# The last 1536 gate columns of the modulation, as running sums on VectorE beside the output projection

## The chip, the cores and the metric

The kernel runs on one core of one Trainium2 chip, in one launch. The metric is the device time of that launch in microseconds (us); lower is better. It is given as the median of several runs, and one further execution is recorded by the profiler.

## The reference

One layer of a diffusion backbone: 384 tokens (128 of a prompt, 256 of a sample) of width 4096, all in float32. A conditioning vector gives shift, scale and gate for the prompt and for the sample; the tokens are normalised and modulated, projected to the inputs of eight retention heads and sixteen delta-rule heads, mixed, and projected back; the gate scales the result before it is added to the tokens.

```python
mod = jax.nn.silu(c) @ w_ada[l] + b_ada[l]           # 2 vectors (c_ctx, c) x [4096, 12288]
shift, scale, gate = jnp.split(mod, 3, axis=-1)
u = _rms_norm(h, norm_w[l]) * (1.0 + scale) + shift
out, states = _mixer(u, ...)                         # u @ w_in, heads, mixed @ w_out
h = h + gate * out
y = _rms_norm(h, final_norm_w)
```

The change concerns the last third of `w_ada`: gate = silu(c) @ w_ada[:, 8192:12288] + b_ada, 4096 columns for two vectors.

## The kernel before

PE (TensorE) does nearly all of the work; a program written in Python sets the order of every instruction on every engine. The unit of this order is a piece, with a `prepare` (loads and splitting) and a `compute` (matmuls). `run_pieces` (L348) calls `prepare` for pieces ahead of the one that computes, until four of them are held (`RING - 1`), so the loads, ACT's and VectorE's steps for a piece stand ahead of its matmuls by up to four chunks.

Stages, in order of time: shift and scale beside the first parts of the input projection (0 to about 790 us); the rest of the input projection in eight pairs of heads, each with its delta-rule and retention steps as background work between the matmuls (about 790 to 2800); the output projection (about 2800 to 3328); the last norm and the stores.

*Products.* float32 products are made of three float32r matmuls. Each chunk of weights (128 rows, 512 columns) is loaded by SP into a `raw` tile that holds two chunks (`load_piece`, L193; four such tiles, `RAW_RING`), cast by ACT into `wh` (L210), and VectorE subtracts to get `wl` (L211): this is called a split here. There are five `wh` and five `wl` buffers (`RING`). In a `Gemm` of kind N the three matmuls L265, L266 and L267 form a triple; a chunk takes three triples, one for each 128 tokens.

*Output projection.* Eight blocks of 512 columns, each a `Gemm` over 32 chunks (L1320). At the end of a block, `rest` (L1300) adds three steps for each 128 tokens on VectorE, `to` (times the gate, L1303), `to`+`xo` (the tokens, L1305) and `hw` (times the norm's weight, L1307), and a square on ACT (L1308); the background clock places them between the next block's splits. The place where one block ends and the next begins is called a joint. `pre` (L1284), five chunks before a block's end, has POOL load `go` (the gate, from `d_gate` in DRAM), `wo` and `xo`. In block 0 the mixed rows are read back from DRAM (`mixl`, L1244) and split into `uh` and `ul` (L1247, L1248), two at a time.

*Gate before.* `Ada` (L302): for 512 columns there are 16 pieces; each loads 512 rows of 256 columns (512 KB, into a `raw` tile) and runs four matmuls of 128x32 by 128x256 in four column groups of the array, with the conditioning vectors (`cst`) as the stationary side (L323). Then ACT copies the sums (L1177), two matmuls with `sel` add the four groups (L1183), POOL loads the bias into `gsb` (L1187), VectorE adds (L1190), POOL stores to `d_gate` (L1191). All eight such blocks lie in the mixer stage, one in each of the eight pairs of heads 0 to 7, spread between the pieces of the kind-N groups (L1213 to L1232).

*Background.* Each pair's delta-rule (`gdn`) and retention (`ret`) steps are generators; `slot` (L186) counts the nominal time of the matmuls issued and takes the next step when the count runs out, and `pace` (L152) shrinks the counts when a due time comes near. `urgent` steps, among them the end of a gate block, go first.

Of the kernel before, what the change touches and what calls it, by code (L numbers as in the profile page):

```python
# [7 lines left out]
F32 = mybir.dt.float32  # L8
# [7 lines left out]
D = 4096  # L16
NK = 32
# [49 lines left out]
def hybrid_step(ctx: ExitStack, tc: tile.TileContext, x_prompt, x_sample, state_ret_fwd, state_ret_bwd,  # L67
# [41 lines left out]
    gnw = mid.tile([128, 1], F32, name="gnw")  # L109
    cst = mid.tile([128, 2 * NK + 32], F32, name="cst")  # L110
    sel = mid.tile([128, 2], F32, name="sel")
# [79 lines left out]


    def load_piece(src, chunks, k0, nk, ring=None):  # L193
        shape = [128, nk, len(chunks), chunks[0][1]]
        if ring:
            raw = ring(shape)
        else:
            raw = wpool.tile(shape, F32, tag="raw", name="raw", bufs=RAW_RING)
        for i, (c0, cn) in enumerate(chunks):
            SP.dma_start(out=raw[:, :, i, :],  # L200
                         in_=src[k0 * 128:(k0 + nk) * 128, c0:c0 + cn].rearrange("(k p) n -> p k n", p=128))
        return raw

    def split_tile(raw, shape, place=None):
        if place:
            h, lo = place
        else:
            h = wpool.tile(shape, F32R, tag="wh", name="wh", bufs=RING)
            lo = wpool.tile(shape, F32R, tag="wl", name="wl", bufs=RING)
        A.copy(h, raw)  # L210
        V.tensor_tensor(lo, raw, h.bitcast(F32), op=ALU.subtract)  # L211
        return h, lo

# [88 lines left out]
    class Ada:  # L302
# [14 lines left out]
        def compute(self, i, raw):  # L317
# [30 lines left out]
    def run_pieces(pieces):  # L348
# [8 lines left out]
        room = {"do": len(pieces), "ada": ADA_RING - 1, "w": RING - 1}  # L357
        kind = lambda o: "do" if isinstance(o, Do) else ("ada" if isinstance(o, Ada) and o.ring else "w")
        for idx, (obj, i) in enumerate(pieces):
# [853 lines left out]
    ada_q = []  # L1213
    for i in range(8):
        ada_q += Ada(2 * D + 512 * i, 512, lambda: ps_main.tile([128, 512], F32, tag="mm3", name="adg"), gate_done(i)).pieces
    for g, (kind, chunks) in enumerate(groups):
# [5 lines left out]
        if kind == "T":  # L1222
            pieces += gm.pieces
        else:
            n, rest = len(gm.pieces), 0
            if g % 2:
                rest = min(8, n // 2)
                cnt = len(ada_q) - 16 * (7 - g // 4)
            else:
                cnt = min(16, max(0, 16 * n // (n + NK - reached.get(g + 1, 0) - 8)))  # L1230
            pieces += gm.pieces[:LEAD] + interleave(gm.pieces[LEAD:n - rest], ada_q[:cnt]) + gm.pieces[n - rest:]
            ada_q = ada_q[cnt:]  # L1232
# [16 lines left out]


    oc = {}

# [27 lines left out]
    def out_done(c0):  # L1280
# [33 lines left out]
    def place(i):  # L1314
# [3 lines left out]
                           for t in (uh, ul)]  # L1318

    for i in range(8):  # L1320
        pre, done = out_done(512 * i)
# [6 lines left out]
        if i == 0:  # L1328
# [4 lines left out]
            for j, piece in enumerate(seq):  # L1333
                for m, fn in ((j - 2, mix_put), (j, mix_load)):
                    if 0 <= m < NK:
                        pieces += Do(lambda m=m, fn=fn: fn(m)).pieces
                pieces.append(piece)
        else:
            pieces += gm.pieces
    run_pieces(pieces)  # L1340
# [52 lines left out]
```

## Time and profile before

| | |
|---|---|
| three timed runs, us | 3339.26 (median), 3338.48 to 3340.51 |
| the profiled execution, us | 3342.99 |
| its span, first to last instruction, us | 3340.9 |
| mean granted clock of TensorE | 0.994 |
| loaded and stored | 626.14 MB, mean 187 GB/s |

In the rows below, L is the line of the kernel's source, PE the matmuls of TensorE, PEld its weight loads, DVE VectorE, ACT ScalarE, POOL GpSimd and SP the engine that issues the weight loads. A group row gives line, engine, operation, output and inputs, shapes and count, then the busy time in us and the mean of one in ns, then the idle time before them and what ended it. A timeline row gives start, length, engine, line and operation; in brackets stands the idle time before it and what it waited for. A row of waits gives who waited for whom, the total in us, how often, and the longest. A row of loads gives the tile and source, the issuing queue, the count, the size and the median time from issue to landing in us.

### The profile page before, as it was taken

The page shows a single profiled execution, that of the slowest core. Times are in us where ns is not written, and L with a number is a line of the kernel's source. Part 1 is how long each engine was busy: PE and PEld are TensorE (multiplying, and loading weights), DVE is VectorE, ACT ScalarE, POOL GpSimd, SP SyncE. Part 2 cuts the span into 40 slices and gives each one's busy share as a digit, 9 for nine tenths or more (in the row PEclk, how much of TensorE's full clock was granted, in tenths as well). Part 3 has the DMA queues.
Part 4 walks back from the last instruction along what each step waited for, and adds up shares of the span by engine and source line. Part 5 has one row for each costly group of instructions (what it writes and reads, how often), then busy time and mean ns, then how long its engine had stood idle before and what let it go on. Part 6 is the DMA issues. An engine that isn't in the chain of part 4 may idle for free. (4 is left out here: it accounts for less than half of the span.)

```text
span 3340.9 us, 51824 instructions
## 1 busy us (share of the span) xinstructions
PE 3256.4 (97%) x19312; PEld 2706.2 (81%) x19312; DVE 1840.7 (55%) x3811; ACT 1198.9 (36%) x2588; POOL 292.2 (9%) x463
## 2 busy tenths in 40 slices
PE   5999999999999999999999999999999999999998
PEld 2778888877699779789789779779779877788887
DVE  2554433335855756754856746746844845444444
ACT  3322222224245235244345245235244334333333
POOL 0000000001101001001011001011000012100000
PEclk9999999999999999999999999999999999999999
DMA  9888998975534554544645645554644556645444
GB/s 304 290 287 272 330 311 266 297 251 159 179 105 135 169 153 149 179 145 140 192 146 152 185 129 156 173 154 147 177 153 141 160 153 188 187 145 170 145 151 170
DMA packets 594236, 626.14 MB, mean 187 GB/s; under 512 B 38978, under 2 KB 577042, under 8 KB 593984
## 3 DMA queue, kind: packets, MB, share of 16 engines
q1 hardware_dynamic: 570096, 551.04, 52.7%
q0 software_dynamic: 23888, 71.79, 7.3%
q8 instruction: 151, 2.47, 0.3%
q14 instruction: 101, 0.83, 0.1%
HBM read 590.37 MB, written 32.33 MB: 186 GB/s over the span
## 5 line engine op out<-in xcount | busy, mean ns | idle before, releaser
L211 DVE TENSOR_TENSOR wl<-raw,wh 128x512 fp32r<-128x512 f32 x1274 | 854.3, 687 | 939.8 <-ACT wh L210 935.8
L210 ACT CAST wh<-raw 128x512 fp32r<-128x512 f32 x1274 | 756.6, 620 | 1350.6 <-DMA raw<-in_w_in_dram 659.0
L265 PE MATMUL mm<-wh,uh 128*128 128x512 f32 x1920 | 784.3, 408 | 9.1 <-ACT rawt L564 5.6
L266 PE MATMUL mm<-wl,uh 128*128 128x512 f32 x1920 | 755.3, 393 | 6.4 <-DVE wl L211 5.8
L267 PE MATMUL mm<-wh,ul 128*128 128x512 f32 x1920 | 752.9, 392 | 0.0
L259 PE MATMUL mm<-uh,wh 128*128 128x384 f32 x2048 | 721.0, 352 | 6.2 <-DVE ul L555 3.8
L261 PE MATMUL mm<-uh,wl 128*128 128x384 f32 x2048 | 689.4, 337 | 0.0
L260 PE MATMUL mm<-ul,wh 128*128 128x384 f32 x2048 | 688.8, 336 | 0.0
L265 PEld LDWEIGHTS mm<-wh,uh 128*128 128x128 f32 x1920 | 362.2, 189 | 141.0 <-issue 48.2
L259 PEld LDWEIGHTS mm<-uh,wh 128*128 128x128 f32 x2048 | 387.3, 189 | 51.2 <-issue 34.6
L266 PEld LDWEIGHTS mm<-wl,uh 128*128 128x128 f32 x1920 | 362.7, 189 | 81.2 <-DVE wl L211 14.1
L267 PEld LDWEIGHTS mm<-wh,ul 128*128 128x128 f32 x1920 | 362.2, 189 | 78.2 <-DVE ul L1248 0.7
L260 PEld LDWEIGHTS mm<-ul,wh 128*128 128x128 f32 x2048 | 387.6, 189 | 3.9 <-issue 2.9
L261 PEld LDWEIGHTS mm<-uh,wl 128*128 128x128 f32 x2048 | 386.8, 189 | 0.0
L854 DVE TENSOR_TENSOR tmp<-M 48x4 f32<-48x4 f32 (+14 forms) x240 | 189.3, 789 | 3.4
L323 PE MATMUL ada<-adar,cst 128*32 128x256 f32 x2048 | 147.5, 404 | 26.9 <-DMA adar<-in_w_ada_dram 26.9
L645 DVE SCALAR_TENSOR_TENSOR acc<-rawt,cw,acc 128x126 f32<-128x126 f32 (+3 forms) x384 | 133.8, 413 | 12.8 <-ACT acc L640 12.8
L266 PE MATMUL o<-wl,uh 128*128 128x512 f32 x354 | 138.1, 390 | 0.2 <-DVE wl L211 0.2
L265 PE MATMUL o<-wh,uh 128*128 128x512 f32 x354 | 138.0, 390 | 0.2 <-ACT wh L210 0.2
L267 PE MATMUL o<-wh,ul 128*128 128x512 f32 x354 | 137.9, 390 | 0.0
L323 PEld LDWEIGHTS ada<-adar,cst 128*32 128x32 f32 x2048 | 53.8, 112 | 92.7 <-DMA adar<-in_w_ada_dram 42.8
L856 DVE TENSOR_REDUCE M<-tmp 48x2 f32<-48x4 f32 (+14 forms) x240 | 121.6, 507 | 8.3
(321 smaller groups left out, 2522.7 us busy)
## 6 DMA issues: line engine op xcount, KB each, us to landing
raw<-in_w_in_dram SPq DMA_DIRECT2D x1028, 256.0 KB, 3.6
adar<-in_w_ada_dram SPq DMA_DIRECT2D x256, 512.0 KB, 5.7
raw<-in_w_ada_dram SPq DMA_DIRECT2D x128, 512.0 KB, 4.3
raw<-in_w_out_dram SPq DMA_DIRECT2D x256, 256.0 KB, 3.1
rawt<-d_part POOLq DMA_DIRECT2D x26, 384.0 KB, 4.3
d_part<-spill POOLq DMA_DIRECT2D x9, 768.0 KB, 7.4
gr<-d_gc POOLq DMA_DIRECT2D x16, 384.0 KB, 7.4
d_mix<-rawt POOLq DMA_DIRECT2D x32, 192.0 KB, 2.8
```

The source lines that it names most:

```text
L210: A.copy(h, raw)
L211: V.tensor_tensor(lo, raw, h.bitcast(F32), op=ALU.subtract)
L259: PE.matmul(ps, wh, high(k), start=st, stop=False)
L260: PE.matmul(ps, wh, low(k), start=False, stop=False)
L261: PE.matmul(ps, wl, high(k), start=False, stop=sp)
L265: PE.matmul(ps, a, h, start=st, stop=False)
L266: PE.matmul(ps, a, lo, start=False, stop=False)
L267: PE.matmul(ps, b, h, start=False, stop=sp)
L323: PE.matmul(self.ps[32 * q:32 * q + 32, cs], cst[:, 2 * k:2 * k + 32], raw[:, q, 0], start=(k < 4), stop=(k >= NK - 4), tile_position=(0, ...
L645: V.scalar_tensor_tensor(out=dst[:, lo:hi], in0=x[:, lo + o:hi + o], scalar=w(t), in1=dst[:, lo:hi], op0=ALU.mult, op1=ALU.add)
L854: V.tensor_tensor(t, M[0:48, 0:i, 0:i].rearrange("p j c -> p c j"), M[0:48, i:i + 1, 0:i].to_broadcast([48, i, i]), op=ALU.mult)
L856: V.tensor_reduce(M[0:48, i, 0:i], t, axis=AX.X, op=ALU.add)
```

## The change

The first 2560 gate columns stay as they are: five `Ada` blocks, now in the pairs 1, 2, 4, 5 and 6 (`GATE_PAIRS`). The last 1536 become four `GateSum`s of 384 columns. Each has 16 pieces; a piece loads 256 rows of 384 columns (384 KB) into a `raw` tile, and for each of its two 128-row chunks VectorE multiplies the chunk by a column of `cst` and adds it to a running sum, one for each of the two vectors (`gacc`). The two instructions for one chunk are called an add pair. The first pair of a piece is issued at once, the second after the next split (`later`). After 16 pieces four matmuls with `ones`, in four column groups, sum over the partitions (L382, `gsum`); POOL loads the bias into the running sum's tile (L386), VectorE adds (L388), POOL stores to `d_gate`. The pieces are interleaved with the chunks of blocks 1 to 6 of the output projection, one for every three chunks. `cst` and `oc` move to where both stages see them.

```diff
+GATE_W = 384
+GATE_PE = 5
+GATE_PAIRS = (1, 2, 4, 5, 6)
...
     def split_tile(raw, shape, place=None):
...
         A.copy(h, raw)
         V.tensor_tensor(lo, raw, h.bitcast(F32), op=ALU.subtract)
+        if later:
+            later.pop(0)()
         return h, lo
...
+    class GateSum:
+        slots = 0.0
+        def __init__(self, c0):
+            self.c0 = c0
+            self.pieces = [(self, i) for i in range(0, NK, 2)]
+        def prepare(self, i):
+            raw = load_piece(w_ada, [(2 * D + self.c0, GATE_W)], i, 2)
+            if i == 0:
+                self.acc = [oc["sb"].tile([128, GATE_W], F32, tag=f"ga{v}", name="gacc", bufs=2) for v in range(2)]
+            def add(q):
+                for v, acc in enumerate(self.acc):
+                    w = cst[:, 2 * (i + q) + v:2 * (i + q) + v + 1]
+                    if i + q == 0:
+                        V.tensor_scalar(acc, raw[:, q, 0], scalar1=w, scalar2=None, op0=ALU.mult)
+                    else:
+                        V.scalar_tensor_tensor(out=acc, in0=raw[:, q, 0], scalar=w, in1=acc, op0=ALU.mult, op1=ALU.add)
+            while later:
+                later.pop(0)()
+            add(0)
+            if i + 2 < NK:
+                later.append(lambda: add(1))
+            else:
+                add(1)
+        def compute(self, i, hl):
+            if i + 2 == NK:
+                urgent.append(self.fin())
+            return 1
+        def fin(self):
+            n, sb = GATE_W // 2, self.acc[0]
+            parts = [(32 * q, q // 2, n * (q % 2)) for q in range(4)]
+            yield GATE
+            ps = ps_main.tile([128, n], F32, tag="mm3", name="gsum")
+            for r, v, o in parts:
+                PE.matmul(ps[r:r + 32], ones, self.acc[v][:, o:o + n], start=True, stop=True, tile_position=(0, r))
+            yield
+            for r, v, o in parts:
+                c0 = 2 * D + self.c0 + o
+                G.dma_start(out=sb[r:r + 32, 0:n], in_=b_ada[0, c0:c0 + n].partition_broadcast(32))
+            yield 2000
+            V.tensor_tensor(sb[:, 0:n], ps, sb[:, 0:n], op=ALU.add)
+            for r, v, o in parts:
+                G.dma_start(out=d_gate[v:v + 1, self.c0 + o:self.c0 + o + n], in_=sb[r:r + 1, 0:n])
...
-    for i in range(8):
+    for i in range(GATE_PE):
         ada_q += Ada(2 * D + 512 * i, 512, ...).pieces
...
-                cnt = len(ada_q) - 16 * (7 - g // 4)
+                cnt = len(ada_q) % 16
             else:
-                cnt = min(16, max(0, 16 * n // (n + NK - reached.get(g + 1, 0) - 8)))
+                cnt = min(16, max(0, 16 * n // (n + NK - reached.get(g + 1, 0) - 8))) if g // 4 in GATE_PAIRS else 0
...
+        elif i < 7:
+            behind += gm.pieces
         else:
-            pieces += gm.pieces
+            gate_sums = [p for c0 in range(512 * GATE_PE, D, GATE_W) for p in GateSum(c0).pieces]
+            pieces += interleave(behind, gate_sums) + gm.pieces
```

Lines of the changed kernel are higher by up to 63: the matmuls of a triple are L276 to L278 there, a split's subtraction L220, `to` L1366, `+xo` L1368, `hw` L1370. A tile's number after its name tells buffers apart.

On PE, in the last group of pair 7, these rows stood before: a late step of the delta rule (L926) and a piece of the last gate block (`adg`) between triples.

```order
L926 MATMUL bg_25192<-U_24209,P2_25180 64x64 x12
L265 MATMUL mm2_25084<-wh_25078,uh1_837 128x512
L266 MATMUL mm2_25084<-wl_25079,uh1_837 128x512
L267 MATMUL mm2_25084<-wh_25078,ul1_838 128x512
L323 MATMUL adg_24527<-raw_25149,cst_82 32x256 x4
L265 MATMUL mm0_25082<-wh_25154,uh2_1310 128x512
L266 MATMUL mm0_25082<-wl_25155,uh2_1310 128x512
L267 MATMUL mm0_25082<-wh_25154,ul2_1311 128x512
```

After the same number of projection matmuls (the triple `mm0` on `uh2` is the same in both) there stand now:

```order
L276 MATMUL mm2_24788<-wh_24782,uh1_839 128x512
L277 MATMUL mm2_24788<-wl_24783,uh1_839 128x512
L278 MATMUL mm2_24788<-wh_24782,ul1_840 128x512
L276 MATMUL mm0_24786<-wh_24835,uh2_1312 128x512
L277 MATMUL mm0_24786<-wl_24836,uh2_1312 128x512
L278 MATMUL mm0_24786<-wh_24835,ul2_1313 128x512
L979 MATMUL bg_24921<-x64_0_7129,U_23990 64x64 x6
L979 MATMUL bg_24921<-x64_1_7130,U_23990 64x64 x6
```

The gate piece is gone, and the delta rule is only at the step L979, which is L916 of before and came ahead of L926 there: in pair 7 its steps stand later among the matmuls.

On VectorE, at the joint of blocks 0 and 1, from the first `to` on, these rows stood before (`wl` is a split):

```order
L1303 TENSOR_TENSOR to_26571<-mm0_25934,go_26505 128x512
L211 TENSOR_TENSOR wl_26580<-raw_26576,wh_26579 128x512
L211 TENSOR_TENSOR wl_26584<-raw_26576,wh_26583 128x512
L1305 TENSOR_TENSOR to_26571<-to_26571,xo_26504 128x512
L1307 TENSOR_TENSOR hw_26501<-to_26571,wo_26506 128x512
L1303 TENSOR_TENSOR to_26611<-mm1_25935,go_26505 128x512
L211 TENSOR_TENSOR wl_26617<-raw_26613,wh_26616 128x512
L211 TENSOR_TENSOR wl_26621<-raw_26613,wh_26620 128x512
L1305 TENSOR_TENSOR to_26611<-to_26611,xo_26504 128x512
L1307 TENSOR_TENSOR hw_26501<-to_26611,wo_26506 128x512
L211 TENSOR_TENSOR wl_26640<-raw_26636,wh_26639 128x512
L1303 TENSOR_TENSOR to_26652<-mm2_25936,go_26505 128x512
```

Now, from the same `to` on:

```order
L1366 TENSOR_TENSOR to_26254<-mm0_25608,go_26180 128x512
L220 TENSOR_TENSOR wl_26263<-raw_26259,wh_26262 128x512
L220 TENSOR_TENSOR wl_26267<-raw_26259,wh_26266 128x512
L362 SCALAR_TENSOR_TENSOR gacc_26220<-raw_26270,cst_74,gacc_26220 128x384
L362 SCALAR_TENSOR_TENSOR gacc_26221<-raw_26270,cst_74,gacc_26221 128x384
L1368 TENSOR_TENSOR to_26254<-to_26254,xo_26179 128x512
L1370 TENSOR_TENSOR hw_26176<-to_26254,wo_26181 128x512
L1366 TENSOR_TENSOR to_26295<-mm1_25609,go_26180 128x512
L220 TENSOR_TENSOR wl_26304<-raw_26300,wh_26303 128x512
L362 SCALAR_TENSOR_TENSOR gacc_26220<-raw_26270,cst_74,gacc_26220 128x384
L362 SCALAR_TENSOR_TENSOR gacc_26221<-raw_26270,cst_74,gacc_26221 128x384
L220 TENSOR_TENSOR wl_26310<-raw_26300,wh_26309 128x512
```

One add pair has come in ahead of the first `xo` step and one between the next two splits; two more follow, one on each side of the third `to`.

On VectorE, at the joint of blocks 3 and 4, these rows stood before, from the two splits ahead of the first `to`:

```order
L211 TENSOR_TENSOR wl_28010<-raw_28006,wh_28009 128x512
L211 TENSOR_TENSOR wl_28023<-raw_28006,wh_28022 128x512
L1303 TENSOR_TENSOR to_28041<-o0_27568,go_27977 128x512
L211 TENSOR_TENSOR wl_28050<-raw_28046,wh_28049 128x512
L211 TENSOR_TENSOR wl_28054<-raw_28046,wh_28053 128x512
L1305 TENSOR_TENSOR to_28041<-to_28041,xo_27976 128x512
L1307 TENSOR_TENSOR hw_26501<-to_28041,wo_27978 128x512
L1303 TENSOR_TENSOR to_28081<-o1_27569,go_27977 128x512
```

Now, from the splits of chunks 2 and 3 of block 4:

```order
L220 TENSOR_TENSOR wl_27946<-raw_27942,wh_27945 128x512
L220 TENSOR_TENSOR wl_27950<-raw_27942,wh_27949 128x512
L362 SCALAR_TENSOR_TENSOR gacc_27900<-raw_27953,cst_74,gacc_27900 128x384
L362 SCALAR_TENSOR_TENSOR gacc_27901<-raw_27953,cst_74,gacc_27901 128x384
L388 TENSOR_TENSOR gacc_27058<-gsum_27934,gacc_27058 128x192
L220 TENSOR_TENSOR wl_27991<-raw_27987,wh_27990 128x512
L362 SCALAR_TENSOR_TENSOR gacc_27900<-raw_27953,cst_74,gacc_27900 128x384
L362 SCALAR_TENSOR_TENSOR gacc_27901<-raw_27953,cst_74,gacc_27901 128x384
L220 TENSOR_TENSOR wl_27997<-raw_27987,wh_27996 128x512
L1366 TENSOR_TENSOR to_28003<-o0_27398,go_27862 128x512
L1368 TENSOR_TENSOR to_28003<-to_28003,xo_27861 128x512
L220 TENSOR_TENSOR wl_28016<-raw_28012,wh_28015 128x512
```

The last step of the second gate sum (L388) stands ahead of the splits of chunks 4 on and of the first `to`, and an add pair between the splits on each side.

More of the change, by code (lines that the diff above doesn't have):

```diff
@@ L103, in hybrid_step @@
     half_c = const.tile([128, 2, 12], F32, name="half_c")
+    ones = const.tile([128, 32], F32, name="ones")
+    cst = const.tile([128, 2 * NK + 32], F32, name="cst")
     mid_ctx = ExitStack()
@@ L109, in hybrid_step @@
     gnw = mid.tile([128, 1], F32, name="gnw")
-    cst = mid.tile([128, 2 * NK + 32], F32, name="cst")
     sel = mid.tile([128, 2], F32, name="sel")
@@ L121, in hybrid_step @@
     rk_dec = mid.tile([128, 2, 8], F32, name="rk_dec")
+    G.memset(ones, 1.0)
     G.memset(half_c[:, 0], -0.5)
@@ L190, in slot @@
             clock["next"] = max(clock["next"], -SLOT) + bg_step()
+    oc = {}
     def load_piece(src, chunks, k0, nk, ring=None):
@@ L202, in load_piece @@
         return raw
+    later = []
     def split_tile(raw, shape, place=None):
@@ L328, in compute @@
             return 1
+    class GateSum:
[40 more added lines that the diff above has]
+                G.dma_start(out=d_gate[v:v + 1, self.c0 + o:self.c0 + o + n], in_=sb[r:r + 1, 0:n])
+            clock["gate"] = self.c0 + GATE_W
     class Do:
@@ L357, in run_pieces @@
         room = {"do": len(pieces), "ada": ADA_RING - 1, "w": RING - 1}
-        kind = lambda o: "do" if isinstance(o, Do) else ("ada" if isinstance(o, Ada) and o.ring else "w")
+        kind = lambda o: "do" if isinstance(o, (Do, GateSum)) else ("ada" if isinstance(o, Ada) and o.ring else "w")
         for idx, (obj, i) in enumerate(pieces):
@@ L1213, in hybrid_step @@
     ada_q = []
-    for i in range(8):
+    clock["gate"] = 512 * GATE_PE
+    for i in range(GATE_PE):
         ada_q += Ada(2 * D + 512 * i, 512, lambda: ps_main.tile([128, 512], F32, tag="mm3", name="adg"), gate_done(i)).pieces
@@ L1248, in mix_put @@
         V.tensor_tensor(low(j), mixl[j], high(j).bitcast(F32), op=ALU.subtract)
-    oc = {}
     def open_out():
@@ L1288, in pre @@
             op = oc["sb"]
+            assert clock["gate"] >= c0 + 512
             box["x"] = op.tile([128, 3, 512], F32, tag="xo", name="xo", bufs=1)
@@ L1318, in place @@
                            for t in (uh, ul)]
+    behind = []
     for i in range(8):
```

## The prediction

> **What bounds the kernel now.** I read the page first (span, busy shares), then busy time by stage, then the waits of the output projection, then the timeline at the two places that the change touches.
>
> ```profile
> span 3340.9 us, 51824 instructions
> PE 3256.4 (97%) x19312; PEld 2706.2 (81%) x19312; DVE 1840.7 (55%) x3811; ACT 1198.9 (36%) x2588; POOL 292.2 (9%) x463
> 1030.00:1280.00 250.00, 250.00 (x1473) 209.62 (x1472) 151.68 (x321) 100.06 (x230) 28.06 (x42) 1.00 0.52 156
> 2530.00:2780.00 250.00, 250.00 (x1492) 212.91 (x1491) 155.91 (x330) 96.81 (x216) 30.03 (x45) 1.00 0.54 164
> 2990.00:3050.00 60.00, 60.00 (x267) 49.74 (x266) 25.89 (x39) 20.19 (x36) 2.87 (x5) 1.00 0.52 158
> ```
>
> Columns of the stage rows: length, busy PE, PEld, DVE, ACT, POOL, granted clock, DMA share, GB/s. PE is busy all of a mixer stage (1030 to 1280) and all of the output projection (2990 to 3050) at a full clock. VectorE works 26 of 60 us in the projection, 152 to 156 of 250 in the mixers. PE's instruction stream is the bound in both; what leaves it is gained, if nothing else then comes late.
>
> ```profile
> DVE wl L211 <- ACT wh L210: 227.5, 178, 2.2
> ACT wh L210 <- PE o L267: 116.5, 84, 2.8
> ACT wh L210 <- PE mm L267: 109.8, 77, 3.3
> SPq L200 <- DVE wl L211: 324.9, 106, 6.7
> ```
>
> These waits of the projection (2870 to 3300) close the loop: VectorE's splits wait for ACT's, ACT waits for PE to give back one of five split buffers, and the loads wait for VectorE to give back one of four raw buffers. All run ahead of PE, by at most four chunks.
>
> **What the change removes from PE.** Three gate blocks, 48 pieces.
>
> ```profile
> 1612.63 0.39 PE L265 MATMUL mm<-wh,uh 128*128 128x512 f32 x1
> 1613.31 0.39 PE L265 MATMUL mm<-wh,uh 128*128 128x512 f32 x1
> 1614.09 0.64 PE L323 MATMUL adg<-raw,cst 128*32 128x256 f32 x8
> 1615.45 0.40 PE L265 MATMUL mm<-wh,uh 128*128 128x512 f32 x1
> 1683.63 0.39 PE L265 MATMUL mm<-wh,uh 128*128 128x512 f32 x1
> 1684.41 1.02 PE L1183 MATMUL adg<-gsb,sel 128*2 128x256 f32 x4
> 1686.16 0.39 PE L265 MATMUL mm<-wh,uh 128*128 128x512 f32 x1
> ```
>
> Matmul ends are modelled, so I take start to start. A triple (L265, L266, L267) lasts 1613.31 - 1612.63 = 0.68. Two triples with a gate piece between last 1615.45 - 1613.31 = 2.14, so the piece costs 0.78: 48 x 0.78 = **37.4 us**. The sum over the row groups (L1183) stands in 1686.16 - 1683.63 = 2.53, less two triples 1.17: three of them, **3.5**. No row before is a gsum; it is four matmuls into four column groups like a gate piece, with 192 columns instead of 256: above by the four one after another (1.17), below nothing; I take 0.7, nearest to the gate piece scaled by 192/256 (0.58): 4 x 0.7 = **2.8** (0 to 4.7). Net on PE: -37.4 - 3.5 + 2.8 = **-38.1**.
>
> The mixers hide chains of small steps beside these pieces. Pairs 0, 3 and 7 lose about 13.6 us each (16 x 0.78 + 1.17). In pair 7 the order puts the delta-rule steps up to 30 matmuls later, 7 us, and the retention steps only 3 to 6. VectorE would do its 156 us in 236 instead of 250: covered, and I charge nothing. SP issues 48 loads of 512 KB less beside them and ACT six copies. If that cover were gone in pair 7, its 13.6 would not be gained.
>
> **What it adds on VectorE.**
>
> ```profile
> L211 DVE TENSOR_TENSOR wl<-raw,wh 128x512 fp32r<-128x512 f32 x177 | 121.6, 692 | 193.0 <-ACT wh L210 192.7
> L1305 DVE TENSOR_TENSOR to<-to,xo 128x512 f32<-128x512 f32 x18 | 12.4, 688 | 0.3
> L645 DVE SCALAR_TENSOR_TENSOR acc<-rawt,cw,acc 128x126 f32<-128x126 f32 x96 | 33.3, 347 | 12.8 <-ACT acc L640 12.8
> L645 DVE SCALAR_TENSOR_TENSOR acc<-rawt,cw,acc 128x255 f32<-128x255 f32 x96 | 46.1, 480 | 0.0
> L1053 DVE SCALAR_TENSOR_TENSOR rawt<-bg,gnw,rawt 128x384 f32<-128x384 f32 x16 | 9.8, 614 | 6.2 <-PE bg L1051 5.8
> L1065 DVE TENSOR_SCALAR Wr<-rcon,lgam 128x384 f32<-128x384 f32 x8 | 3.4, 431 | 0.0
> 3053.75 0.69 DVE L211 TENSOR_TENSOR wl<-raw,wh 128x512 fp32r<-128x512 f32 x1 [1.34 <-ACT wh L210]
> 3055.79 0.69 DVE L211 TENSOR_TENSOR wl<-raw,wh 128x512 fp32r<-128x512 f32 x1 [1.35 <-ACT wh L210]
> ```
>
> The same operation at 126 and 255 elements (347, 480 ns) gives 1.03 ns an element and, at 384, 613; L1053 at that size shows 614. There are 248 of these and 8 first products (431): 152.3 + 3.4 = 156 us over blocks 1 to 6, 26 a block. A chunk takes 3055.79 - 3053.75 = 2.04 us on PE, a block 65.3. VectorE has 32 x 0.692 + 9 x 0.688 = 28.3 there now, so 54.3 of 65.3, 83%. Inside a block it needs 0.69 + 1.33 x 0.61 = 1.5 us of a chunk's 2.04 and can win back lead. On average it is hidden; at the joints between blocks it need not be. SP gets 64 loads of 384 KB between the w_out loads, POOL four small loads and four stores a sum.
>
> ```profile
> 2872.28 0.69 DVE L1303 TENSOR_TENSOR to<-mm,go 128x512 f32<-128x512 f32 x1 [5.75 <-DMA go<-d_gate]
> 2875.76 0.69 DVE L1305 TENSOR_TENSOR to<-to,xo 128x512 f32<-128x512 f32 x1 [1.59 <-DMA xo<-in_x_prompt_dram]
> 2878.56 1.29 DVE L211 TENSOR_TENSOR wl<-raw,wh 128x512 fp32r<-128x512 f32 x2 [0.78 <-ACT wh L210]
> 2887.00 3.10 DVE L211 TENSOR_TENSOR wl<-raw,wh 128x512 fp32r<-128x512 f32 x5 [1.30 <-ACT wh L210]
> 2878.58 0.50 PE L265 MATMUL o<-wh,uh 128*128 128x512 f32 x1 [0.24 <-ACT wh L210]
> ```
>
> **Joint 0 to 1.** Here VectorE first waits for go and xo, and PE, already without lead, waits for ACT at chunk 4 (2878.58). The order now puts four add pairs (1.23 each, 4.9) between the first `to` and the split of chunk 8, which starts at 2887.00 now. One pair falls into the 1.59 us wait for xo; 3.7 are left. Walking the rows one by one, PE waits at chunks 6, 7 and 8: **3.4 us**.
>
> **Joint 3 to 4.** The second sum's last step (L388) stands on VectorE ahead of the splits of chunk 4 on and of all `to`, `xo` and `hw` steps, and waits for four loads that POOL issues only once gsum is done.
>
> ```profile
> L1187 POOL DMA_DIRECT2D gsb<-in_b_ada_dram x16: 499/528/574, 896.8 to 2768.6; - x16
> DMA to landing us min/median/max: 1.5/3.1/4.8
> ```
>
> That is 0.7 + 4 x 0.53 + 3.1 = 6 us after gsum. The same walk from there has PE wait at chunks 9 to 11: **3.5 us**. The sums that end in mid-block (blocks 2 and 5) meet a lead of four chunks, 8 us, and cost nothing; the last one, at joint 6 to 7, has no adds behind it. At the four other joints the walk leaves the split of chunk 8 ready 0.2 to 1.0 us before PE asks: 0.5 each, **2.0**.
>
> **The clock after a wait.**
>
> ```profile
> 2864.73 0.50 PE L265 MATMUL mm<-wh,uh 128*128 128x512 f32 x1 [2.80 <-ACT uh L1247]
> 2866.00:2868.00 2.00, 2.00 (x6) 1.57 (x5) 0.53 (x1) 0.24 (x1) 2.00 (x4) 0.50 0.27 61
> 2869.30 0.40 PE L265 MATMUL mm<-wh,uh 128*128 128x512 f32 x1
> ```
>
> After a wait of 2.80 us PE was granted half its clock: from 2864.73 to 2869.30 stand four triples, 4.57 us instead of 2.72, so 1.9 lost on top. My waits at the joints are up to 2.1 us in one piece; I add one such loss, **2.0** (0 to 6). [...]
>
> **Sum.** -38.1 + 3.4 + 3.5 + 2.0 + 2.0 = **-27.2**. The profiled execution took 3342.99 (span 3340.9 and 2.1 around it) and would take 3316; the median of the three timed runs is 3339.26, 3.7 less, so on that scale **3312**.
>
> **Rivals.** (1) No waits at the joints: VectorE's waits there now (0.78, 1.30 at two splits above) absorb the adds, and the wait of 2.80 us for the last mixed rows with its slow clock (4.7 together) goes too, since the first loads of these rows no longer stand behind the last gate block's store on POOL. For it: the margins are near 1 us. Against: PE has no lead at joint 0 to 1, and the loads of these rows lag later by their own chain. Time: 3339.3 - 38.1 = 3301, down to 3297. (2) The mixer chains bind in pair 7 (or 0): 13.6 not gained, 3326. For it: the steps there stand later. Against: the order keeps all other pairs within a few matmuls.
>
> (3) Slower: the raw ring. Five raw tiles pass in six chunks (three of w_out, two of w_ada) through four buffers, and VectorE's queue stops at an add whose tile hasn't landed, with all splits behind it.
>
> ```profile
> raw<-in_w_out_dram SPq DMA_DIRECT2D x103, 256.0 KB, 3.0
> xo<-in_x_sample_dram POOLq DMA_DIRECT2D x6, 256.0 KB, 7.3
> raw<-in_w_ada_dram SPq DMA_DIRECT2D x14, 512.0 KB, 4.3
> ```
>
> A buffer's round is landing plus about 3.5 us (ACT, split, pair, split); 5/4 rounds must fit in 6 x 2.04 = 12.2, so landing may be 6.3. At 4.3, as w_ada loads land beside the mixers, there are 2.5 us to spare in 12.2. From 6.3 on each further us costs 1.25 in each of the 32 rounds, 40 us; past 7.3, the time of xo's loads in the same stage, the whole 38 us is gone and at 7.8 the kernel takes about 3360. For it: loads rise from 158 to some 220 GB/s here, with bursts of 1.5 MB at each joint. Against: the mixer stretch with gate pieces moved 218 GB/s at a landing of 4.3.
>
> ```profile
> 1614.10:1681.40 67.30, 66.04 (x363) 45.31 (x362) 55.50 (x93) 13.69 (x24) 5.03 (x9) 1.00 0.72 218
> ```
>
> (4) It doesn't do what it says: ring and joints together give back most of the 38, and the time stays within 0.2% (6.7 us, about what a measurement of this kernel can tell from no change).
>
> **Chances.** Forecast (3305 to 3320) 0.50; rival 1 0.20; rival 2 0.12; part of rival 3 or more clock losses, 3320 to 3332, 0.07; rival 4 0.05; slower by rival 3 0.06. So faster by over 0.2% 0.89, the same 0.05, slower 0.06. The range takes rival 1 down to 3299 and the others up to 3330.
>
> **What would show it.** L323 falls from 3072 to 2688 matmul rows; gacc rows near 0.61 us; VectorE near 50 of 60 us inside blocks 1 to 6; PE waits for wl or wh at joints 0 to 1 and 3 to 4 of 3 to 4 us each, few elsewhere; a granted clock below 1 at one joint. Wrong if the raw w_ada loads land after 6 us or more, if gacc rows last over 0.75 us (VectorE then fills its block), or if PE waits in pair 7.

## The result and the profile after

| | us |
|---|---|
| before, median of 5 runs | 3338.78 (3338.33 to 3340.51) |
| after, median of 5 runs | **3322.55** (3317.74 to 3325.22) |
| after / before | 0.9946, 95% interval 0.9934 to 0.9959 |
| profiled execution, before and after | 3342.99 and 3321.15 (spans 3340.9 and 3319.4) |

The change saves 16.2 us in the medians; 27.2 were forecast (3312, with a range of 3299 to 3330). First the head of the page of after and its busy shares, then three stages, the groups of the sums, their loads and one pair of adds in the timeline; the columns are those of before.

```profile
span 3319.4 us, 51468 instructions
PE 3217.4 (97%) x18948; PEld 2690.6 (81%) x18948; DVE 1965.9 (59%) x4065; ACT 1196.0 (36%) x2582; POOL 301.3 (9%) x484
```

```profile
1030.00:1280.00 250.00, 249.29 (x1467) 208.23 (x1466) 147.80 (x309) 98.11 (x226) 28.05 (x42) 1.00 0.52 155
2990.00:3050.00 60.00, 58.15 (x254) 46.97 (x253) 39.18 (x69) 18.16 (x31) 3.94 (x8) 0.97 0.62 196
2850.00:3240.00 390.00, 383.23 (x1690) 311.90 (x1689) 279.36 (x481) 120.40 (x220) 28.79 (x54) 1.00 0.69 215
```

```profile
L362 DVE SCALAR_TENSOR_TENSOR gacc<-raw,cst,gacc 128x384 f32<-128x384 f32 x248 | 141.4, 613 | 5.0 <-DMA raw<-in_w_ada_dram 5.0
L360 DVE TENSOR_SCALAR gacc<-raw,cst 128x384 f32<-128x384 f32 x8 | 3.2, 440 | 0.0
L382 PE MATMUL gsum<-gacc,ones 128*32 128x192 f32 x32 | 2.1, 338 | 0.0
```

```profile
raw<-in_w_ada_dram SPq DMA_DIRECT2D x64, 384.0 KB, 4.2
```

```profile
2840.87 1.14 DVE L362 SCALAR_TENSOR_TENSOR gacc<-raw,cst,gacc 128x384 f32<-128x384 f32 x2
```

PE, which was busy all 60 us of the projection stage, now misses 1.85 us there, and its granted clock fell from 1.00 to 0.97. The adds last 613 ns, as forecast. VectorE went from 26 to 39 of 60 us in this stage; from 2850 to 3240, nearly all of blocks 1 to 6, it has 279.36 of 390 us, 72%, where 83% was forecast. The forecast counted every instruction at its full duration; neighbours overlap (two adds of 613 ns take 1.14 us together).

The waits of PE, and two of ACT, which feeds it, from 2830 to 3270 (us in total, times, longest):

```profile
ACT wh L219 <- DMA raw<-in_w_out_dram: 128.9, 46, 8.8
ACT to L1371 <- DVE hw L1370: 79.5, 21, 8.4
PE o L276 <- ACT wh L219: 3.3, 3, 1.6
PE mm L276 <- ACT wh L219: 2.0, 3, 1.0
PE o L277 <- DVE wl L220: 1.9, 5, 1.0
PE mm L277 <- DVE wl L220: 1.2, 4, 0.5
```

**Where the time went, stage by stage.** All 13152 projection matmuls (of `w_in` and `w_out`) stand in the same order in both kernels, and every one is in the trace. So the time from one of them to a later one, start to start, can be compared between any two runs, whatever happened earlier. The mixer stage begins at matmul 2880; its 7968 matmuls are cut into eight equal parts, "pair 0" to "pair 7" (the cuts are near the pairs' own ends). A block of the projection has 288. The second column of before is the profile of experiment e4.

| us | before | before, 2nd | after | after less the mean of before |
|---|---|---|---|---|
| start of the first projection matmul | 59.7 | 58.4 | 63.7 | +4.7 |
| first stage, from there to pair 0 | 704.2 | 697.3 | 702.4 | +1.7 |
| pair 0 | 260.5 | 259.5 | 247.4 | **-12.6** |
| pairs 1 and 2 | 508.6 | 508.0 | 509.2 | +0.9 |
| pair 3 | 233.3 | 233.2 | 226.3 | **-7.0** |
| pairs 4, 5 and 6 | 777.7 | 778.6 | 774.5 | -3.7 |
| pair 7 | 247.4 | 247.2 | 233.6 | **-13.7** |
| block 0 | 78.4 | 74.8 | 73.5 | -3.1 |
| block 1 | 66.6 | 68.2 | 71.1 | +3.7 |
| block 2 | 65.3 | 65.3 | 66.0 | +0.7 |
| block 3 | 65.3 | 65.3 | 69.9 | +4.6 |
| block 4 | 65.3 | 65.3 | 67.7 | +2.4 |
| block 5 | 65.3 | 65.3 | 66.0 | +0.7 |
| block 6 | 65.3 | 65.3 | 68.9 | +3.6 |
| block 7 and the end | 77.9 | 77.9 | 79.4 | +1.5 |
| from pair 0 to the end | 2577.0 | 2573.8 | 2553.3 | **-22.1** |

Three things are to be explained: pair 3 gives half of what pairs 0 and 7 give; blocks 1, 3, 4 and 6 wait; and the first stage, in which no work was changed, is later.

### The profile page after: what moved, and what is told of

It reads as the page before. It is cut to its first block, busy times and chain, and to the rows that moved or that the text cites. A ratio compares the mean times of both kernels' runs of the same rounds, so it can differ in the third digit from the quotient of the medians.

```text
span 3319.4 us, 51468 instructions
## 1 busy us (share of the span) xinstructions
PE 3217.4 (97%) x18948; PEld 2690.6 (81%) x18948; DVE 1965.9 (59%) x4065; ACT 1196.0 (36%) x2582; POOL 301.3 (9%) x484
## 5 line engine op out<-in xcount | busy, mean ns | idle before, releaser
L220 DVE TENSOR_TENSOR wl<-raw,wh 128x512 fp32r<-128x512 f32 x1274 | 850.8, 686 | 788.9 <-ACT wh L219 769.8
L276 PE MATMUL mm<-wh,uh 128*128 128x512 f32 x1920 | 776.8, 405 | 9.3 <-ACT rawt L627 4.9
L278 PE MATMUL mm<-wh,ul 128*128 128x512 f32 x1920 | 749.6, 390 | 0.0
L276 PEld LDWEIGHTS mm<-wh,uh 128*128 128x128 f32 x1920 | 360.5, 188 | 124.2 <-issue 32.3
L278 PEld LDWEIGHTS mm<-wh,ul 128*128 128x128 f32 x1920 | 360.5, 188 | 76.9
L917 DVE TENSOR_TENSOR tmp<-M 48x4 f32<-48x4 f32 (+14 forms) x240 | 189.5, 790 | 3.3
L334 PE MATMUL ada<-adar,cst 128*32 128x256 f32 x2048 | 148.7, 406 | 29.0 <-DMA adar<-in_w_ada_dram 29.0
L362 DVE SCALAR_TENSOR_TENSOR gacc<-raw,cst,gacc 128x384 f32<-128x384 f32 x248 | 141.4, 613 | 5.0 <-DMA raw<-in_w_ada_dram 5.0
L276 PE MATMUL o<-wh,uh 128*128 128x512 f32 x354 | 138.9, 392 | 3.4 <-ACT wh L219 3.3
L278 PE MATMUL o<-wh,ul 128*128 128x512 f32 x354 | 138.3, 391 | 0.0
L334 PEld LDWEIGHTS ada<-adar,cst 128*32 128x32 f32 x2048 | 53.7, 112 | 96.2 <-DMA adar<-in_w_ada_dram 45.9
```

Of the source, the lines that this page charges most:

```text
L276: PE.matmul(ps, a, h, start=st, stop=False)
L278: PE.matmul(ps, b, h, start=False, stop=sp)
L334: PE.matmul(self.ps[32 * q:32 * q + 32, cs], cst[:, 2 * k:2 * k + 32], raw[:, q, 0], start=(k < 4), stop=(k >= NK - 4), tile_position=(0, ...
L362: V.scalar_tensor_tensor(out=acc, in0=raw[:, q, 0], scalar=w, in1=acc, op0=ALU.mult, op1=ALU.add)
L917: V.tensor_tensor(t, M[0:48, 0:i, 0:i].rearrange("p j c -> p c j"), M[0:48, i:i + 1, 0:i].to_broadcast([48, i, i]), op=ALU.mult)
```

## The experiments

### The projection's waits: loads, adds, or both

The two suspects at the blocks' beginnings are VectorE's add pairs (theory A) and the loads (theory B). The rows for theory A are in block 1:

```profile
2849.89 0.69 DVE L1370 TENSOR_TENSOR hw<-to,wo 128x512 f32<-128x512 f32 x1
2850.62 0.63 ACT L1371 ACTIVATE to<-to 128x512 f32<-128x512 f32 x1 [4.88 <-DVE hw L1370]
2851.24 1.12 ACT L219 CAST wh<-raw 128x512 fp32r<-128x512 f32 x2
2851.90 0.50 PE L276 MATMUL o<-wh,uh 128*128 128x512 f32 x1 [1.53 <-ACT wh L219]
```

The block before ends with to, xo and hw on VectorE and a square on ACT. Theory A reads the rows so: with add pairs between them, hw comes late; ACT stands 4.88 us at its square, the copy wh stands behind the square, and PE waits for the copy. For theory B, the answer on DMA for 20 us in block 3 (2976 to 2996; size, median us to landing):

```profile
raw<-in_w_out_dram SPq DMA_DIRECT2D x8, 256.0 KB, 5.1
raw<-in_w_ada_dram SPq DMA_DIRECT2D x2, 384.0 KB, 8.3
go<-d_gate POOLq DMA_DIRECT2D x1, 512.0 KB, 8.7
xo<-in_x_sample_dram POOLq DMA_DIRECT2D x2, 256.0 KB, 8.3
...
```

POOL issues the five loads for the end of the block as soon as their buffers come free, in block 3 some 12 us after its beginning: 512 KB of go, 256 of wo and three times 256 of xo, 1.5 MB at once (the expectations say 1.28, which is too low), and w_ada tiles that land after 4.2 us elsewhere take 8.3.

**e1, no sums.** `prepare` of GateSum loads nothing and adds nothing:

```diff
-            raw = load_piece(w_ada, [(2 * D + self.c0, GATE_W)], i, 2)
...
+                for acc in self.acc:
+                    G.memset(acc, 0.0)
+            return
```

> The changed kernel without the 64 loads of w_ada and without the 256 adds of the running sums (the sums are zero, so the last 1536 gate columns are the bias alone); the four gsum groups, the bias loads and the stores stay. Theory A (VectorE's adds make the last steps hw late, ScalarE stands at its square and the wh copies behind it are late) and theory B (the five loads of xo, go and wo, 1.28 MB, fall together with the w_ada loads and the w_out tiles land late) both expect the same here: of the 13.8 us that the tensor engine loses in blocks 1 to 7 of the changed kernel (4.5 at joint 0 to 1, 3.9 in block 3, 2.4 in block 4, 3.0 in block 6) at most 1 is left, so about 3309 us in the median (3322.5 less 13). If the sums cost through something else than the adds and the loads (the stores, the gsum groups), the waits stay and the time is above 3318. The mixer stages are untouched, so the 5 us that pairs 0 and 3 wait more for wl than before should be there again.

**e2, loads only.** As e1, with the load, and each pair of adds replaced:

```diff
+                V.tensor_copy(self.acc[0][:, 0:1], raw[:, q, 0, 0:1])
```

> The changed kernel with the 64 loads of w_ada in the same raw buffers, but each add pair replaced by a copy of one element (the last 1536 gate columns are left out but for the bias). Theory A expects no waits beyond 1 us at joint 0 to 1: about 3309 to 3310. Theory B expects the 3.9 us in block 3 and the 3.0 in block 6 to stay, the waits at joint 0 to 1 and in block 4 to go: about 3316.

**e3, adds only.** As e1, with the adds reading the other sum:

```diff
+                    V.scalar_tensor_tensor(out=acc, in0=self.acc[1 - v], scalar=w, in1=acc, op0=ALU.mult, op1=ALU.add)
```

> The changed kernel with 256 adds of the same shape in the same places, read from the other sum's tile in SBUF instead of from a loaded tile, and no load of w_ada (the last 1536 gate columns are left out but for the bias). Theory A expects the waits at joint 0 to 1 (4.5) and in block 4 (2.4) to stay and those of blocks 3 and 6 to go: about 3316. If all waits come from the loads (B alone): 3309. If all come from the adds (A alone): 3322.

| us | after | e1 neither | e2 loads | e3 adds |
|---|---|---|---|---|
| block 1 | 71.1 | 66.9 | 69.1 | 73.4 |
| block 2 | 66.0 | 66.0 | 66.0 | 66.0 |
| block 3 | 69.9 | 66.0 | 66.0 | 66.0 |
| block 4 | 67.7 | 65.3 | 65.3 | 68.3 |
| block 6 | 68.9 | 66.0 | 66.0 | 66.0 |
| pair 3 | 226.3 | 227.0 | 225.3 | 227.0 |
| from pair 0 to the end | 2553.3 | 2541.1 | 2541.8 | 2551.4 |
| median of the runs | 3322.55 | 3311.4 | 3309.3 | 3318.0 |

PE's waits from 2826 to 3262 in e1 (one line) and in e3 (four):

```profile
PE o L277 <- DVE wl L220: 0.7, 1, 0.7
```

```profile
PE o L277 <- DVE wl L220: 2.3, 2, 2.0
PE o L276 <- ACT wh L219: 1.7, 1, 1.7
PE mm L277 <- DVE wl L220: 1.0, 2, 0.8
PE mm L276 <- ACT wh L219: 0.9, 1, 0.9
```

The gsum groups, bias loads and stores by themselves cost 0.7 us a sum (66.0 instead of 65.3 in blocks 2, 3, 5 and 6); block 7 keeps its 79.4. Block 4 needs the adds and no load: theory A. Blocks 3 and 6 wait only with both: theory B as it was written, in which the loads alone are enough there, fell. The reading that fits is that the burst makes the tiles late, and that this reaches PE only because VectorE, with adds to do, cannot run ahead of it. Block 1 loses 2.2 us with the loads alone and 6.5 with the adds alone, but both numbers are partly made by the edits: VectorE stood 3.29 us in e2 and 3.65 in e3 at its first step on the sums until POOL had cleared them. So block 1 is not divided between loads and adds by these runs.

**e4, the kernel before again.** No edit.

> The kernel before, unchanged, for a second profile. 3339 us. If the 4.7 us that the first profile of it lost at the last mixed rows (a wait of 2.80 us and the half clock behind it) belong to the kernel, they are there again; if they were an accident of that execution (3342.99 against a median of 3338.8), they are gone and the profiled execution is nearer to 3339. The half clock in the first 100 us (20 us long in the first profile of before, 48 us in that of the changed kernel) should differ from run to run if it is no part of the change.

3336.21 us (median of 12), ratio 0.9989, interval 0.9981 to 0.9998. In its profile block 0 takes 74.8 us instead of 78.4 and the first stage 6.9 us less. So 3.6 us at the last mixed rows in the first profile were an accident of that execution: PE waits 0.9 us there in the second one instead of 2.8, and behind the 2.8 the first one lost 1.9 more at a granted clock of 0.50. Up to pair 0 the first profile was 8.2 us longer than the second one of the same program. The medians of the same program, too, differ by 3.9 us here (3340.06 for the 17 runs taken beside these 12), with an interval that leaves out 1. So differences of a few us are judged by the stages, not by the medians.

**e5, the square one step later.**

```diff
             V.tensor_tensor(oc["hw"][:, n, cs], t, box["w"], op=ALU.mult)
+            yield
             A.activation(t, t, AF.Square, accum_out=oc["sq"][:, n, c0 // 512:c0 // 512 + 1])
```

> The changed kernel with one step more between the last product hw and ScalarE's square of it, so that ScalarE's copies wh no longer stand behind a square that waits 3 to 8 us for hw. Theory A in its form with ScalarE's queue (the square is what makes wh late) expects block 1 to fall from 71.1 us to below 69 and block 4 from 67.7 to about 66.2; blocks 3 and 6 unchanged (69.9, 68.9): 3 us less in all, about 3319.5. If VectorE itself is what is late there (its queue full of add pairs), block 1 stays at 71 and block 4 at 67.7: 3322.5.

Block 1 took 70.5 us and block 4 67.4: a miss. It doesn't decide between the two readings, because one step was too little to free ACT's queue. In block 1 ACT still stands at three squares, for 7.73, 4.97 and 3.31 us, with copies right behind them; the first:

```profile
2844.24 0.63 ACT L1372 ACTIVATE to<-to 128x512 f32<-128x512 f32 x1 [7.73 <-DVE hw L1370]
2844.87 1.64 ACT L219 CAST wh<-raw 128x512 fp32r<-128x512 f32 x3
```

That VectorE itself is what is late is argued, not shown. Blocks 3 and 6 fell to 67.4 and 67.7, which was not expected, but this can't be put down to the edit: e9, which leaves the projection as in after, has 67.7 and 66.2. In after, e8, e9 and e10, all with the same projection, block 3 took 69.9 (with a granted clock of 0.50 from 2994.5 to 2997.5), 70.6, 67.7 and 69.9 us, and block 6 took 68.9, 67.7, 66.2 and 67.8. Median 3317.4, from pair 0 on 2548.5.

**e6, the five loads apart.** They leave `pre` and go on SP's queue, one every second chunk from chunk 14 of their block:

```diff
+            if j >= XO_AT and j % 2 == 0 and (j - XO_AT) // 2 < 5:
+                out += Do(lambda m=(j - XO_AT) // 2: load(m, SP)).pieces
```

> The changed kernel with the five loads of go, wo and xo of blocks 1 to 7 issued one by one between the w_out loads of the same block (chunks 14 to 22) on SyncE's queue instead of together on GpSimd's as soon as their buffers come free. Theory B (their 1.28 MB in one burst make the raw tiles late, and both the adds and the splits on VectorE then stand) expects blocks 3 and 6 to fall from 69.9 and 68.9 us to 66 or 66.5, blocks 1 and 4 unchanged (71.1, 67.7): 6 us less, about 3316.5. If the w_ada loads alone crowd the ring (no burst needed), blocks 3 and 6 stay where they are.

Blocks 3 and 6: 66.0 each, nothing left; block 1 the same (71.2), block 4 69.3, 1.6 more than in after, which stays open, and block 7 with the end 77.8 instead of 79.4. The loads in the same 20 us:

```profile
raw<-in_w_out_dram SPq DMA_DIRECT2D x9, 256.0 KB, 3.2
raw<-in_w_ada_dram SPq DMA_DIRECT2D x3, 384.0 KB, 4.1
```

With e1 to e3 this settles block 3: burst and adds together. Block 6 behaves alike, but without any edit it took as little as 66.2 (e9). Burst and adds are not enough by themselves, though: in blocks 2 and 5, where the burst stands behind POOL's part of a gate sum and comes 40 us after the joint instead of 12, they cost nothing beyond the sum's 0.7. Block 2 of after begins at 2901.5 and block 3 at 2967.5; the first loads of their bursts:

```profile
2941.07 0.76 POOL L1355 DMA_DIRECT2D go<-d_gate  x1
2979.80 0.71 POOL L1355 DMA_DIRECT2D go<-d_gate  x1 [35.85 <-DVE to L1366]
```

The median of e6 is 3317.9.

**e7, no gate pieces in the first eight chunks.**

```diff
+            for b, ps in enumerate(behind):
+                n, gs = (11, gate_sums[11 * b:11 * b + 11]) if b < 5 else (9, gate_sums[55:])
+                pieces += ps[:8] + interleave(ps[8:len(ps) if b < 5 else 26], gs) + ([] if b < 5 else ps[26:])
-            pieces += interleave(behind, gate_sums) + gm.pieces
+            pieces += gm.pieces
```

> The changed kernel with the 64 gate pieces kept out of the first eight chunks of each block (11 in each of blocks 1 to 5, 9 in block 6), so that the last steps of the block before (to, xo, hw, the square) are done before the adds begin. Theory A expects block 1 at about 67 us and block 4 at 66; theory B expects the burst in blocks 3 and 6 to pass before the adds begin, so 66 there too: together 10 us less, about 3312. Against it: inside the rest of the block the adds are then denser (VectorE 89% instead of 83%, three raw tiles in less than four chunks), and if the ring cannot carry that, every block loses 2 us or more.

Blocks 1, 3, 4 and 6: 68.7, 66.0, 65.5 and 66.0; the ring carries the denser adds. Block 1 was expected at 67: PE still waits there, 1.9 us in all. Median 3311.3, ratio 0.9922 (0.9909 to 0.9935).

### The mixers: why pair 3 gives half

Each pair has 30 steps of growing size on VectorE (L917 a product, L919 a reduction: the inverse of 32-row blocks), called the chain here. In pair 3 of after they take 39 us of VectorE within 51.5 us:

```profile
1646.22 1.02 DVE L919 TENSOR_REDUCE M<-tmp 48x29 f32<-48x841 f32 x1
1646.77 0.62 ACT L219 CAST wh<-raw 128x512 fp32r<-128x512 f32 x1 [2.00 <-PE mm L278]
1647.16 1.27 DVE L220 TENSOR_TENSOR wl<-raw,wh 128x512 fp32r<-128x512 f32 x2
1647.89 0.50 PE L277 MATMUL mm<-wl,uh 128*128 128x512 f32 x1 [0.92 <-DVE wl L220]
1648.36 1.82 DVE L917 TENSOR_TENSOR tmp<-M 48x900 f32<-48x900 f32 x1
```

The copy is ready, but the split stands behind a step of the chain and PE waits for wl. A gate piece needs no split, so it was PE work that lies beside this chain for free: this is theory C.

**e8, half blocks in seven pairs.** Ten gate blocks of 256 columns (8 pieces each):

```diff
-GATE_PAIRS = (1, 2, 4, 5, 6)
+GATE_HALVES = (1, 2, 1, 1, 2, 1, 2, 0)
```

> The changed kernel with the 2560 gate columns of TensorE cut into ten blocks of 256 instead of five of 512, one or two in each of pairs 0 to 6 (1, 2, 1, 1, 2, 1, 2, and none in pair 7). Theory C (beside the 30 steps L917/L919, where VectorE works 92 to 97% of 50 us, the gate pieces are work for TensorE that needs no split from VectorE; without them TensorE waits for wl) expects pair 3, 491 us before and after less only 8, to gain back some 5 us of wl waits, while pairs 1, 4 and 6 hardly change: about 3317.5. The rival, that pair 3's loss is from the order in which the delta-rule steps stand (their due times), expects no change in the sum of the eight pairs (1991.0 us).

3328.2 us, from pair 0 on 2560.8, 7.5 more than after: the expectation failed. Eight pieces, 6.2 us of PE work, came back into pair 3 and it grew by 3.5 (229.8), so some cover was bought back; but pair 0 grew by 8.4 (255.8), where the clock was at half for 6.8 us behind a wait of 4.2, and PE waited ahead of gate pieces (L334), which it had not done in after: 1.0 us for a matmul, 2.2 for VectorE's step of the gate sum before, 1.9 in issue. It does not decide theory C; it showed that pair 2 gives all of a half block (247.4 instead of 255.3), and that pair 5 gives next to nothing for the same eight pieces (256.3 instead of 256.9), which stays open.

**e9, other pairs.**

```diff
-GATE_PAIRS = (1, 2, 4, 5, 6)
+GATE_PAIRS = (1, 3, 4, 5, 6)
```

> The changed kernel with the five gate blocks of TensorE in pairs 1, 3, 4, 5, 6 instead of 1, 2, 4, 5, 6, so that pair 2 and not pair 3 goes without. If what a removed gate block is worth depends on the pair (pair 0 gave 13.1 and pair 7 13.8 us, pair 3 only 7.0, and taking half a block out of pair 2 gave 7.9 in the run with half blocks), the stage of pair 3 returns from 226.3 to 233 us and that of pair 2 falls from 255.3 to about 242: 6.6 us less, 3316. If any pair in the middle loses half of it to waits for wl, pair 2 falls only to 248.5 and the time stays at 3322.

Pair 3 went back to 234.1 (+7.8) and pair 2 fell to 243.1 (-12.2). What a block is worth depends on the pair that loses it: 12 to 14 us in pairs 0, 2 and 7, 7 in pair 3. Median 3313.2, from pair 0 on 2545.8. Of the 7.5 us less than after, 3.2 lie in the eight pairs; the rest lies in the projection, which the edit leaves as it was.

**e10, pair 3 without its 30 steps.**

```diff
+            if p == 3:
+                yield 390.0 + 2.1 * i * i
+                continue
             t = tmp[0:48, 0:i * i].rearrange("p (c j) -> p c j", j=i)
```

> The changed kernel without the 30 steps L917/L919 (a product and a reduction each) in pair 3 alone, their places in the order kept; the inverse of the delta rule's 32-row blocks is left out for these two heads. Theory C (beside these steps VectorE has no time for the splits, and what TensorE no longer does in gate pieces it waits) expects the stage of pair 3 to fall from 226.3 to 218 to 220 us (233.3 less 13.6, less up to 1.5 of the wait that was there before), so 3315 in the median. If the missing 6.6 us are due to another place in that pair (the delta-rule steps behind it, or loads), it stays at 226.

Pair 3 took **218.4** us, as theory C expected. The stage rows around the chain of pair 3 of before, of after and of e10 (length, PE, PEld, VectorE):

```profile
1614.00:1668.00 54.00, 52.74 (x286) 36.48 (x285) 49.94 (x82) 10.50 (x19) 0.00 (x0) 1.00 0.67 210
```

```profile
1600.00:1655.00 55.00, 52.34 (x225) 41.33 (x223) 50.56 (x84) 15.80 (x26) 0.30 (x1) 1.00 0.38 112
```

```profile
1600.00:1655.00 55.00, 55.00 (x246) 45.68 (x245) 20.83 (x34) 17.37 (x28) 8.62 (x16) 1.00 0.52 154
```

VectorE has 50.56 of 55 us in after and 20.83 without the chain; PE goes from 52.34 to all 55. The missing 7 us of pair 3 are the chain's, but only in part by the way that theory C names. PE's waits in pair 3 of after (1560 to 1760) were 6.2 us, against 1.3 before and 0.6 in e10; the two longest rows:

```profile
PE mm L277 <- DVE wl L220: 3.2, 5, 1.3
PE mm L276 <- ACT rawt L627: 2.4, 1, 2.4
```

The first is theory C's wait for wl. The second comes at 1665.9, 11 us after the chain: ACT copies finished sums away late, in turns with VectorE, whose queue had stood 5.55 us at a later step of the delta rule (L931) until a load landed. About 2 us of the loss stand in no row of waits and stay unexplained.

VectorE being nearly full is not enough for the loss, either. Beside the same chain in pair 7 of after, which has no gate pieces, VectorE has 53.12 of 55 us, and PE is busy all 55:

```profile
2600.00:2655.00 55.00, 55.00 (x244) 45.26 (x243) 53.12 (x87) 17.10 (x28) 0.00 (x0) 1.00 0.38 115
```

Why pairs 2 and 7 can carry the same chain was not tried. Median 3316.9.

### The edits together

**e11** joins e6, e7 and the pairs of e9.

> Three edits together on the changed kernel: gate pieces out of the first eight chunks of each block, the loads of go, wo and xo one by one on SyncE's queue, and the gate blocks in pairs 1, 3, 4, 5, 6. If they add up by stages: block 1 from 71.1 to 67.5 to 68.7, block 3 from 69.9 to 66, block 4 from 67.7 to 65.5, block 6 from 68.9 to 66, block 7 from 79.4 to 77.8 (12.5 to 13.5 less), and the pairs 6.6 less if pair 2 gives all of its block: 3303, otherwise 3309.

3309.4 us in the median of 6 (3304.5 to 3319.3). Block 3, 4 and 6: 66.0, 65.3, 66.4; block 7 77.8; pairs 2 and 3 243.1 and 234.3. From pair 0 on 2538.7, 14.6 less than after, where 19 to 20 were expected with a pair 2 that gives its whole block: a miss, though pair 2 did. Block 0 took 75.7 instead of 73.5, where PE waits 0.8 us for the last mixed rows again, and block 1 stayed at 70.9, over what was expected. VectorE's first step there, and what PE then waits for:

```profile
2832.76 0.69 DVE L1376 TENSOR_TENSOR to<-mm,go 128x512 f32<-128x512 f32 x1 [7.12 <-DMA go<-d_gate]
```

```profile
PE o L278 <- DVE wl L221: 3.8, 1, 3.8
```

**e12** is e11 with block 0's first step held back.

```diff
         def rest(n, ps):
-            yield
+            yield 5000 if n + c0 == 0 else None
```

> The three edits of the run before, and the first step of block 0's last steps (the product of the sums with go) issued some 7 us later, behind more splits. In the run before TensorE waits 3.8 us for wl at the start of block 1 because VectorE's queue stands 7.1 us at this product, until go has landed, with the splits behind it. If that queue is what joint 0 to 1 still costs, block 1 falls from 70.9 to 66.0 to 67.0 us and nothing else changes: 4 to 5 us less, a span of about 3301. If the late landing of go only shifts the wait to the steps behind it (hw late, the copies wh late), block 1 stays above 69.

Block 1: 68.5, half of what was hoped for: the wait behind `go` is gone, and 0.9 us for wh and 0.5 for wl came some chunks later, so that the block ends between the two forecasts. **3306.5 us** (median of 6, 3303.0 to 3314.0), ratio 0.9906 (0.9890 to 0.9923): faster than the changed kernel, whose interval lies above. From pair 0 on it takes 2537.4 us, 15.9 less.

### What stays open: the first stage

The change leaves the first stage's work as it was, but all kernels made from the changed one start their first projection matmul at 61.1 to 64.5 us (twelve profiles), the two profiles of before at 59.7 and 58.4. PE waits for the loads of adar there. Four of its groups, in before and in after:

```profile
21.29 1.08 PE L323 MATMUL ada<-adar,cst 128*32 128x256 f32 x8 [1.55 <-DMA adar<-in_w_ada_dram]
23.89 1.08 PE L323 MATMUL ada<-adar,cst 128*32 128x256 f32 x8 [1.52 <-DMA adar<-in_w_ada_dram]
```

```profile
22.82 1.08 PE L334 MATMUL ada<-adar,cst 128*32 128x256 f32 x8 [1.92 <-DMA adar<-in_w_ada_dram]
25.68 1.08 PE L334 MATMUL ada<-adar,cst 128*32 128x256 f32 x8 [1.78 <-DMA adar<-in_w_ada_dram]
```

A load of 512 KB lands every 2.60 us before and every 2.86 after, 10% slower; the second profile of before has 2.60 as well (26.88 to 29.48), and e3 and e12 2.86. The medians agree: in each of the twelve kernels the gain by medians is 2 to 10 us smaller than the gain from pair 0 on, for the change itself 16.2 against 22.1. So about **6 us** are lost ahead of pair 0. Some 4 of them lie before the first projection matmul (63.1 us in the mean of the twelve, 59.1 of the two); behind it the twelve take 700.9 to 708.0 us up to pair 0 and the two 697.3 and 704.2, which overlap. The author's guess at a cause for the first part is the place of the tiles: the change moves `cst` and `ones` ahead of the other tiles. No run here shows that the place decides how fast the adar loads land; an edit that moves only these tiles back would test it and was not tried, so the cause stays open.

## Why the prediction was right or wrong, point by point

- **Direction and range** held. Of the 11.0 us by which the gain was too large, 5.1 lie from pair 0 on (22.1 instead of 27.2), and about 6 in the first stage.
- **48 gate pieces and three sums less, -40.9.** The eight pairs took 2027.6 and 2026.5 us before and 1990.9 after: 36.2 less than their mean. The step that failed is "covered, and I charge nothing". It compared VectorE's 156 us with 236 us of the stage; in pair 3 the cover was needed in and just behind the 50 us of the chain, where VectorE has over 90%. There PE's waits grew from 1.3 to 6.2 us, the pair gave 7.0 of 13.6, and without the chain it gives the rest (e10). Rival 2 had the mechanism in the wrong pair: it named 7 or 0, and pair 7 gave its 13.6 in full (13.7), with as full a VectorE; why stays open.
- **gsum, +2.8.** Four times 0.7: right (e1).
- **Adds of 0.61 us, landing below 6 us.** 613 ns and 4.2 us: right, though in the burst of block 3 the tiles took 8.3. VectorE's load was over-sized (72% against 83%).
- **Joint 0 to 1, 3.4.** 3.7 against the mean of before (66.6 and 68.2). e1 shows that it goes with the sums (66.9). The four pairs between the splits are not all of it: with no adds in the first eight chunks the block still takes 68.7 (e7) and 70.9 (e11).
- **Joint 3 to 4, 3.5.** 2.4, at the chunks forecast. But it is not L388's wait alone: e1 keeps L388 and its bias loads and has 65.3. Without the adds behind it, it costs nothing.
- **The four other joints, 0.5 each.** Wrong in place and size: nothing in blocks 2 and 5, and 3.9 and 2.9 us in blocks 3 and 6, 20 to 27 us behind the joint. The walk took loads as landing at their mean. Rival 3 had the bursts, with a price for every round; what came was a loss at two bursts. The two sizes are those of one execution: with the same projection e9 has 67.7 and 66.2 us there, 1.7 and 0.2 more than 66.0.
- **Clock, 2.0.** One spell at a granted clock of 0.50 in block 3, inside its 3.9 us, and not at a joint; see below.
- **Rival 1's 4.7 us at the last mixed rows.** The wait went, as the rival had it, but most of its 4.7 us belonged to that one execution: block 0 is 3.6 us shorter in e4. Set against this, block 7 ends 1.5 us later, which was not forecast and goes with the loads apart (e6).
- **The sum of the projection.** 2.8 + 10.9 = 13.7 us forecast, 14.1 measured from block 0 to the end: near, but through errors that cancel.
- **The scale.** 3.7 us were taken off for the profile's distance from the median. That was fair for before; the loss in the first stage was seen by no step, since "nothing changed there".

## What to carry to other kernels

Take cover stage by stage: work moved off the busiest engine need not give its full time, and the mean over a long stage does not show it. In pair 3 half was lost in and behind the 50 us of a serial chain on VectorE; in pair 7, with the same chain, nothing was, so a full neighbour is a warning and no price. Before adding steady loads, look for bursts that were harmless so far (here they came with w_ada tiles that took 8.3 us instead of 4.2), and for steps at which a queue stands with others behind them (VectorE's stood 7.12 us at one in e11); spreading five loads, and keeping the adds out of eight chunks, each took away the waits in blocks 3 and 6. And compare stages between the same instructions, in more than one profile: a stage that was "not touched" can move by 6 us, and two profiles of one program differed by 11 in their spans (3340.9 and 3329.5).

## What the runs showed of the hardware that was not expected

A wait of 1.62 us, shorter than the 2.80 us of the first profile, was followed by half a clock too. In block 3 of after (start, length, and the idle time before):

```profile
2993.77 0.50 PE L276 MATMUL o<-wh,uh 128*128 128x512 f32 x1 [1.62 <-ACT wh L219]
2994.50 0.79 PE L277 MATMUL o<-wl,uh 128*128 128x512 f32 x1 [0.23 <-DVE wl L220]
2995.09 0.63 PE L278 MATMUL o<-wh,ul 128*128 128x512 f32 x1
2995.51 0.63 PE L276 MATMUL o<-wh,uh 128*128 128x512 f32 x1
...
2997.65 0.46 PE L278 MATMUL o<-wh,ul 128*128 128x512 f32 x1
```

From 2995.09 on the matmuls start 0.43 us apart instead of 0.23, for 2.6 us; the granted clock was 0.50 from 2994.5 to 2997.5. A wait of 1.53 in block 1 had no such effect (1.00 from 2850 to 2856), nor had the one of 2.42 in pair 3 (1.00 from 1664 to 1670). So in this execution the length of a wait alone does not decide it; what else counts was not shown.
